# Sixteen score products and sixteen value products of the sample rows, one behind each K tile of the last two input blocks

## The chip, the cores and the metric

The kernel runs on one core of one Trainium2 chip. The metric is device time in microseconds, the median of three runs before. A profile of one execution stands beside it.

## The reference

One step of a hybrid decoder layer in fp32. A prompt (512 tokens behind 16 meta tokens) and eight sample rows share all weights. What matters here:

```python
z = h @ w_in + b_in                       # q (16 heads x 64) | k, v (4 x 64 each) | pool input u (1024)
# sample rows: one new token each against 128 cached keys and itself, with a sink per head
s = einsum('...qhgd,...shd->...hgqs', q, k_all) / 8
p = softmax over keys and the sink
a_s = einsum('...hgqs,...shd->...qhgd', p, v_all)
# prompt: the same in banded blocks of 128 queries; pool branch: trailing means of u over 2, 4, 8, 16, a linear map per group
h = LN(alpha*h + concat(attn, pool) @ w_o);  h = LN(alpha*h + SwiGLU(h))
```

## The kernel before

All dense products are made in three parts: a weight tile is split into `wh` and `wl` (ScalarE copies to fp32r, VectorE subtracts), activations likewise, and `products` (L200 to L206) issues wh x hi, wh x lo and wl x hi as fp32r matmuls, on lines 203, 204 and 206. `full_block` runs one block of 128 output columns over 16 K tiles: four groups of four, each group behind its own split. It holds two outputs, the two halves of the 536 token columns (276 and 260), so a K tile is six matmuls. With `apart=True` it runs all 16 K tiles for the first half and then all 16 for the second; only u7 does so.

The input stage makes k and v first and then eight q blocks (`q0` to `q7`, `q_block`) and eight pool blocks (`u0` to `u7`, `u_block`), in the order written in `order`. Between the blocks stand the steps of the prompt's attention: at each turn t of the loop at the end of the stage `att_values(t - 1)` (tile o, L609), `att_scores(t)` (tile sc, L547), the softmax on VectorE and ScalarE, then the block, then `att_turn(t)` (transposes of the probabilities, tile tp, L591 to L598). `pool_group` (tile pm) is the pool branch's linear map. `u_block` yields behind its block and VectorE's chain (u7 once more, between its two halves); called again, it transposes the last columns of u for an output (tile tpu, L657 and L658).

`with step(pe)` puts everything that TensorE gets inside it behind the step before. Inside a step, and on the other engines and on SP's queue, the order is settled by the planner that the kernel is built with, by program order, a priority for weight loads and splits, and its own estimate of what is ready.

`sample_attention` is a generator in stages, called with `next(sample)` at fixed places:

1. before u6: loads the K cache (`kc`, two loads), makes 16 score products (tile smT, L697: weights 128x128 of the cache, 8 columns moving), copies them out (L699);
2. behind u6 and `att_turn(6)`: transposes the scores (tile smp, L708, L709) and makes the softmax;
3. before u7: transposes the probabilities (tile smpt, L729, L730), copies them to pT (L732), loads the V cache (`vc`, two loads);
4. behind u7 and `att_turn(7)`: 32 value products in 16 pairs (tile smo, L742: weights 128x64 of the cache, 4 columns moving, the two of a pair on different halves of the output's partitions), and the sum (L748);
5. copies the result into the first eight columns of `mixf`, the operand of the output projection.

These products are plain fp32; each shows as two records on TensorE. The loads of weights and caches share a ring of five buffers (`raw`, `NRAW = 5`), taken in turn: kc, kc, u6, u6, pool group 2, vc, vc, u7, u7, pool group 3, w_o. PSUM has eight banks; the code asks for tags `mm` (2), `sc` (4), `pt` (1) and `o` (1), and the tool that lays out the tiles may give a tag another bank when one is free.

Of the kernel before, what the change touches and what calls it, by code (L numbers as in the profile page):

```python
# [16 lines left out]
KT = D // P  # L17
# [50 lines left out]
def hybrid_step(ctx, tc, xin, w_in, w_o, w_g, w_u, w_d, w_pool, par_d, cst_d, ident_d, ln2gb, kct_d, vc_d, hist_d,  # L68
# [136 lines left out]
        for j, o in enumerate(out):  # L205
            nc.tensor.matmul(o, wl, hi[j], start=False, stop=last, skip_group_check=onto)  # L206

    def full_block(src, name, out, hi, lo, low=None, apart=False):


        def mm(w, g, js):
            for kk in range(4):
                k = g * 4 + kk
                sl = slice(kk * P, (kk + 1) * P)
                products([out[j] for j in js], w[0][:, sl], w[1][:, sl], [hi(k)[j] for j in js], [lo(k)[j] for j in js],
                         k == 0, k == KT - 1)

        js = list(range(len(out)))
        ws = []
        for h in range(2):  # L220
            raw = load_raw(src[:, h * 1024:(h + 1) * 1024], f"{name}_{h}")
            for g in range(2):
                ws.append(split(raw[:, g * 512:(g + 1) * 512], f"{name}_{h}{g}", low))
                mm(ws[-1], 2 * h + g, js[:1] if apart else js)
        if apart:
            for g in range(4):
                mm(ws[g], g, js[1:])
# [27 lines left out]
    with ExitStack() as sa:  # L255
# [6 lines left out]
        def aux_tile(shape, tag, name, bufs):  # L262
            return ps.tile(shape, F32, tag=tag, name=name, bufs=bufs)
# [84 lines left out]
        xlo = [act.tile([P, KT, xw[h]], F32R, name=f"xlo{h}") for h in range(2)]  # L348
# [32 lines left out]
                y = y[:, :, META:]  # L381
            last.append(nc.sync.dma_start(h_d[ks, :, HALF[h]].rearrange("k p c -> p k c"), y).ins)

        def in_block(i, name, c0=0, apart=False):

            halves, cs = (0, 1), (slice(c0, xw[0]), slice(0, xw[1]))
            out = [mm_tile(f"mm_{name}_{h}")[:, cs[h]] for h in halves]
            full_block(w_in[i], name, out, lambda k: [xhi[h][:, k, cs[h]] for h in halves],
                       lambda k: [xlo[h][:, k, cs[h]] for h in halves], apart=apart)
            return out  # L390

        def rope(z, dst, name, c0=0):
# [43 lines left out]
        out = kv_banks(0)  # L436
# [4 lines left out]
        for h in range(2):  # L441
            for g in range(4):
                n = h * 4 + g + 1
# [27 lines left out]
            with step(*three):  # L471
# [6 lines left out]
                if h == 0:  # L478
                    out = kv_banks(1)
# [131 lines left out]
            nc.vector.tensor_copy(mixf[t][:, NS:NTOK], o.rearrange("p a b -> p (a b)"))  # L611


        def u_block(ub, apart=False):


            w = 2 << (ub // 2)
            hist = pa.tile([P, NS, POOLH], F32, tag="hist", name=f"hist{ub}", bufs=2)
            with tc.issue_after(last[-1]):
                nc.sync.dma_start(hist, hist_d[ub])  # L620
            out = in_block(12 + ub, f"u{ub}", apart=apart)
            u = pa.tile([P, C_ALL], F32, tag="u", name=f"u{ub}", bufs=2)
            bias = par[:, PBIAS + 12 + ub:PBIAS + 13 + ub]
            cur = [u] + [zt_tile(f"ws{ub}_{i}") for i in range(ub // 2 + 1)]
            if apart:
                d = pa.tile([P, NTOK], F32, name=f"d{ub}")
            else:
                d = zt_tile(f"d{ub}")
            dh = pa.tile([P, NTOK], F32R, tag="dh", name=f"dh{ub}", bufs=3)
            dl = pa.tile([P, NTOK], F32R, tag="dl", name=f"dl{ub}", bufs=3)  # L630
            dd[ub] = dh, dl
            for h, (c0, c1) in enumerate(((C_P, XN), (XN, C_ALL)) if apart else ((C_P, C_ALL),)):
                if h == 0:
                    nc.vector.tensor_scalar(u[:, NS:C_P], out[0][:, 0:META], bias, None, op0=ALU.add)
                    nc.vector.tensor_scalar(u[:, 0:NS], out[0][:, C_S:C_P], bias, None, op0=ALU.add)
                    nc.vector.tensor_scalar(u[:, C_P:XN], out[0][:, C_P:XN], bias, None, op0=ALU.add)
                if c1 == C_ALL:
                    nc.vector.tensor_scalar(u[:, XN:C_ALL], out[1], bias, None, op0=ALU.add)
                for i in range(1, len(cur)):
                    sh = 2 ** (i - 1)  # L640
                    a = c0 if h else NS + 2 ** i - 1
                    nc.vector.tensor_add(cur[i][:, a:c1], cur[i - 1][:, a:c1], cur[i - 1][:, a - sh:c1 - sh])
                nc.vector.scalar_tensor_tensor(d[:, c0 - META:c1 - META], cur[-1][:, c0:c1], 1.0 / w, u[:, c0:c1],
                                               op0=ALU.mult, op1=ALU.subtract)
                if h == 0:
                    hs = pa.tile([P, NS], F32, tag="hs", name=f"hs{ub}", bufs=2)
                    nc.vector.tensor_reduce(out=hs, in_=hist[:, :, POOLH + 1 - w:POOLH], op=ALU.add, axis=AX.X)
                    nc.vector.tensor_add(hs, hs, u[:, 0:NS])
                    nc.vector.scalar_tensor_tensor(d[:, 0:NS], hs, 1.0 / w, u[:, 0:NS], op0=ALU.mult, op1=ALU.subtract)
                ds = slice(c0 - META if h else 0, c1 - META)  # L650
                nc.scalar.copy(dh[:, ds], d[:, ds])
                nc.vector.tensor_sub(dl[:, ds], d[:, ds], dh[:, ds].bitcast(F32))
                if c1 < C_ALL:
                    yield
            yield
            tp = aux_tile([P, 512], "pt", f"tpu{ub}", 1)
            nc.tensor.transpose(tp[:POOLH, 0:P], u[:, C_ALL - POOLH:C_ALL], ident)  # L657
            nc.tensor.transpose(tp[:NS, P:2 * P], u[:, 0:NS], ident)  # L658
            uo = pa.tile([P, 2, P], F32, tag="uo", name=f"uo{ub}", bufs=1)
            nc.scalar.copy(uo[:POOLH, 0], tp[:POOLH, 0:P])  # L660
            nc.scalar.copy(uo[:NS, 1], tp[:NS, P:2 * P])
            us = slice(ub * P, (ub + 1) * P)
            nc.sync.dma_start(npp[:, us], uo[0:POOLH, 0, :])
            nc.sync.dma_start(nps[:, POOLH - 1, us], uo[0:NS, 1, :])
            yield
# [22 lines left out]
        def sample_attention():  # L688

            kcs = [load_raw(kct_d[:, 1024 * i:1024 * (i + 1)], f"kc{i}").rearrange("p (b t s) -> p b t s", b=4, t=2)  # L690
                   for i in range(2)]
            st_ = aux_tile([P, 2, 8, NS], "pt", "smT", 1)
            for b in range(NS):
                kc = kcs[b // 4][:, b % 4]
                for t4 in range(2):
                    ts = slice(4 * t4, 4 * t4 + 4)
                    nc.tensor.matmul(st_[:, :, ts, b], kc[:, t4, :], qd[:, :, ts, b], start=True, stop=True)  # L697
            sT = pa.tile([P, 2, 64], F32, tag="smT", name="sT")
            nc.scalar.copy(sT.rearrange("p j n -> p (j n)"), st_.rearrange("p j t b -> p (j t b)"))  # L699
            prod = pa.tile([P, 8, NS], F32, tag="smp", name="prod")  # L700
# [27 lines left out]
            for j in range(2):  # L728
# [3 lines left out]
            nc.scalar.copy(pT.rearrange("p j t b -> p (j t b)"), pp[:, 0:192])  # L732
            vcs = [load_raw(vc_d[:, 1024 * i:1024 * (i + 1)], f"vc{i}").rearrange("p (b f) -> p b f", b=4)
                   for i in range(2)]
            yield
            so = aux_tile([P, 8, NS], "pt", "smo", 1)
            for b in range(NS):
                vc = vcs[b // 4][:, b % 4]
                for t4 in range(2):
                    for j in range(2):  # L740
                        kv = 2 * t4 + j
                        nc.tensor.matmul(so[64 * j:64 * j + 64, 4 * t4:4 * t4 + 4, b], vc[:, kv * 64:kv * 64 + 64],  # L742
                                         pT[:, j, 4 * t4:4 * t4 + 4, b], start=True, stop=True)
            sv = pa.tile([P, 8, NS], F32, tag="sv", name="sv")
            for i in range(2):
                ts = slice(4 * i, 4 * i + 4)
# [8 lines left out]
        pe = nc.tensor  # L755
        qs, us = {}, []

        def block(n):
            with step(pe):
                if n[0] == "q":  # L760
                    qs[int(n[1])] = q_block(int(n[1]))
                else:
                    us.append(u_block(int(n[1]), n == "u7"))
                    next(us[-1])

        sample = sample_attention()
# [3 lines left out]
        for t in range(8):  # L770
            with step(pe):
                if t:
                    att_values(t - 1)
                sc = att_scores(t, qs.pop(t))
                if t >= 6:
                    next(sample)
            att_softmax(t, sc)
            done, us = us, []
            names = order[t].split()
            block(names[0])  # L780
            with step(pe):
                if t < 7:
                    att_turn(t)
                for u in done:
                    next(u)
                if t == 6:
                    next(sample)
            if t in (3, 5, 6):
                with step(pe):
                    next(pool_group((t - 2) // 2))  # L790
            for name in names[1:]:
                block(name)
        with step(pe):
            att_turn(7)
            next(sample)
        g3 = pool_group(3, True)
        for p in range(2):
            with step(pe):
# [338 lines left out]
    pe = nc.tensor  # L1137
# [387 lines left out]
```

## Time and profile before

| | |
|---|---|
| median of 3 runs | 1921.79 us (1921.46 to 1921.79) |
| the profiled execution | 1923.03 us |
| its span, first to last instruction | 1921.2 us |
| TensorE (PE) busy | 1890.5 us, 98% |
| VectorE (DVE) busy | 1537.7 us, 80% |
| ScalarE (ACT) busy | 957.6 us, 50% |
| mean granted TensorE clock | 0.993 |
| score products (smT) | 295.3 to 299.8 us |
| u6 | 299.8 to 314.0 us |
| u7 | 324.2 to 336.1 us |
| value products (smo) | 338.2 to 340.1 us |

A row of a timeline reads: start, duration (both us), engine, line, operation, output <- input by the program's names, rows*columns of the array used, shape of what moves, count; neighbours of one kind are merged into one row. PE is TensorE's products, PEld its weight loads, which run beside products; SPq is SP's queue of DMAs. A matmul's duration is modelled and contains its way through the array, so consecutive ones overlap; the distance from start to start tells what one costs.

### The profile page before, as it was taken

Reading aid. Unit: us, or ns where it says so; the run is one execution under the profiler, and the core shown is the slowest. Engines: PE = TensorE matmul, PEld = TensorE weight load, DVE = VectorE, ACT = ScalarE, POOL = GpSimd, SP = SyncE. Lnnn points to the kernel's source line nnn. Section 1 sums busy time; section 2 is a strip of 40 time slices with the busy share of each in tenths; the row PEclk is TensorE's granted clock in tenths of the full one; section 3 lists DMA queues with packets and bytes.
Section 4 is the critical chain, followed back from the end, with each engine's and each line's share of the span. In section 5 each row is a group of like instructions: output and inputs, shape, how many; then the busy total and the mean of one; then the engine's idle time right before and its main releaser. Section 6 shows DMA issues by size and latency. Waiting matters only on the chain.

```text
span 1921.2 us, 39215 instructions
## 1 busy us (share of the span) xinstructions
PE 1890.5 (98%) x15533; PEld 1862.9 (97%) x15533; DVE 1537.7 (80%) x2734; ACT 957.6 (50%) x1808; POOL 2.7 (0%) x9
## 2 busy tenths in 40 slices
PE   8999999999999999999999999999999999999996
PEld 8999999999989999999999999999999999999996
DVE  6666667768777988988898888888877888888878
ACT  6644445545654555555555555555555433434341
POOL 0000000000000000000000000000000000000000
PEclk9999999999999999999999999999999999999998
DMA  8722222665745455454545344453568655645332
GB/s 281 233 99 68 70 75 71 206 207 193 251 153 176 150 171 172 148 183 145 176 149 172 128 164 151 153 169 127 178 243 322 233 197 178 219 166 191 94 100 90
DMA packets 145240, 319.27 MB, mean 166 GB/s; under 512 B 14288, under 2 KB 66232, under 8 KB 144952
## 3 DMA queue, kind: packets, MB, share of 16 engines
q1 hardware_dynamic: 144480, 315.71, 49.6%
q8 instruction: 122, 2.00, 0.4%
q10 hardware_dynamic: 576, 1.05, 0.2%
q14 instruction: 62, 0.51, 0.1%
HBM read 265.22 MB, written 54.03 MB: 166 GB/s over the span
## 4 chain that ended last, share of the span: by engine, by line
PE 92%; DVE 3%; DMA 2%; ACT 2%; issue 1%; SPq 0%; DVEq 0%; ACTq 0%
PE p_g L203 8%; PE p_g L204 8%; PE p_g L206 8%; PE p_u L203 7%; PE p_u L206 7%; PE p_u L204 7%; PE tri L203 6%; PE tri L206 6%; PE tri L204 6%; PE o L203 3%; PE o L206 3%; PE o L204 3%; PE p_u L1003 2%; PE mm_u L203 2%; PE mm_u L206 2%; PE mm_u L204 2%
## 5 line engine op out<-in xcount | busy, mean ns | idle before, releaser
L187 ACT CAST rr<-fr 128x512 fp32r<-128x512 f32 (+1 forms) x1056 | 669.9, 644 | 738.3 <-DVE fr L196 151.5
L188 DVE TENSOR_TENSOR rr<-fr,rr 128x512 fp32r<-128x512 f32 (+1 forms) x1056 | 743.7, 715 | 244.2 <-ACT rr L187 233.8
L196 DVE TENSOR_TENSOR fr<-fr 128x1024 f32<-128x1024 f32 (+1 forms) x304 | 319.2, 1050 | 4.9 <-DMA fr<-in_w_g_dram 4.3
L203 PE MATMUL p_g<-rr 128*128 128x260 f32 x830 | 234.1, 283 | 0.0
L206 PE MATMUL p_g<-rr 128*128 128x260 f32 x830 | 230.2, 282 | 0.0
L204 PE MATMUL p_g<-rr 128*128 128x260 f32 x788 | 221.4, 282 | 0.0
L203 PE MATMUL p_u<-rr 128*128 128x260 f32 x770 | 217.8, 283 | 0.6 <-ACT fr L1044 0.6
L206 PE MATMUL p_u<-rr 128*128 128x260 f32 x770 | 214.7, 281 | 0.0
L204 PE MATMUL p_u<-rr 128*128 128x260 f32 x748 | 210.5, 282 | 0.0
L206 PE MATMUL tri<-rr 128*128 128x260 f32 x696 | 196.7, 283 | 1.8 <-DVE rr L188 1.8
L203 PE MATMUL tri<-rr 128*128 128x260 f32 x696 | 197.1, 283 | 0.8 <-ACT rr L187 0.8
L204 PE MATMUL tri<-rr 128*128 128x260 f32 x696 | 196.7, 283 | 0.0
L203 PEld LDWEIGHTS p_g<-rr 128*128 128x128 f32 x830 | 156.1, 188 | 0.0
L206 PEld LDWEIGHTS p_g<-rr 128*128 128x128 f32 x830 | 155.1, 189 | 0.0
L204 PEld LDWEIGHTS p_g<-rr 128*128 128x128 f32 x788 | 148.1, 188 | 0.0
L203 PEld LDWEIGHTS p_u<-rr 128*128 128x128 f32 x770 | 144.8, 188 | 0.8 <-ACT fr L1044 0.8
L203 PE MATMUL o<-rr 128*128 128x260 f32 x512 | 145.0, 284 | 0.3 <-ACT rr L187 0.3
L206 PEld LDWEIGHTS p_u<-rr 128*128 128x128 f32 x770 | 144.4, 189 | 0.0
L204 PE MATMUL o<-rr 128*128 128x260 f32 x512 | 144.0, 282 | 0.0
L206 PE MATMUL o<-rr 128*128 128x260 f32 x512 | 143.6, 282 | 0.2 <-DVE rr L188 0.2
L204 PEld LDWEIGHTS p_u<-rr 128*128 128x128 f32 x748 | 140.6, 188 | 0.0
L206 PEld LDWEIGHTS tri<-rr 128*128 128x128 f32 x696 | 131.3, 189 | 2.6 <-DVE rr L188 2.6
(320 smaller groups left out, 4563.2 us busy)
## 6 DMA issues: line engine op xcount, KB each, us to landing
fr<-in_w_u_dram SPq DMA_DIRECT2D x100, 512.0 KB
fr<-in_w_g_dram SPq DMA_DIRECT2D x90, 512.0 KB
fr<-in_w_d_dram SPq DMA_DIRECT2D x64, 640.0 KB
t_d<-fr SPq DMA_DIRECT2D x140, 260.0 KB
fr<-in_w_o_dram SPq DMA_DIRECT2D x64, 512.0 KB
fr<-in_w_in_dram SPq DMA_DIRECT2D x48, 512.0 KB
rr<-t_d SPq DMA_DIRECT2D x87, 260.0 KB
mid_b<-t_d SPq DMA_DIRECT2D x53, 260.0 KB
```

What stands on the lines that cost most here:

```text
L187: nc.scalar.copy(wh, s)
L188: last_lo[0] = (lo or nc.vector).tensor_sub(wl, s, wh.bitcast(F32)).ins
L196: i = op(*args).ins
L203: nc.tensor.matmul(o, wh, hi[j], start=first, stop=False, skip_group_check=onto)
L204: nc.tensor.matmul(o, wh, lo[j], start=False, stop=False, skip_group_check=onto)
L206: nc.tensor.matmul(o, wl, hi[j], start=False, stop=last, skip_group_check=onto)
L1003: nc.tensor.matmul(bk, self.q(0, n - 1)[:, k * P:(k + 1) * P], z1[0][4 * (n - 1) + k // 2][:, k % 2, :], start=(k == 0), stop=(k == 7))
```

## The change

The generator yields after every single score product, and after every pair of value products, and `full_block` gets an argument `side`: it calls `next(side)` behind each K tile. u6 and u7 pass the generator. In u6 the 16 calls issue one score product each. In u7, which has 32 calls, the first 16 meet bare yields (`KT + 1` of them, the first for the call ahead of the block), and the second 16 issue one pair of value products each. The copy of the scores and the sum of the values follow in a call behind the block. The loads of the K cache stay ahead of u6, those of the V cache ahead of u7 in program order. Because the value products now come inside u7, the tail transposes of u6 (tpu) move: from behind u7 to ahead of it, behind the transposes of the probabilities. `att_turn(7)` no longer has the value products behind it.

```diff
-    def full_block(src, name, out, hi, lo, low=None, apart=False):
+    def full_block(src, name, out, hi, lo, low=None, apart=False, side=None):
...
                 products([out[j] for j in js], w[0][:, sl], w[1][:, sl], [hi(k)[j] for j in js], [lo(k)[j] for j in js],
                          k == 0, k == KT - 1)
+                if side is not None:
+                    next(side)
...
             kcs = [load_raw(kct_d[:, 1024 * i:1024 * (i + 1)], f"kc{i}").rearrange("p (b t s) -> p b t s", b=4, t=2)
                    for i in range(2)]
+            yield
             st_ = aux_tile([P, 2, 8, NS], "pt", "smT", 1)
             for b in range(NS):
                 kc = kcs[b // 4][:, b % 4]
                 for t4 in range(2):
                     ts = slice(4 * t4, 4 * t4 + 4)
                     nc.tensor.matmul(st_[:, :, ts, b], kc[:, t4, :], qd[:, :, ts, b], start=True, stop=True)
+                    yield
...
-            yield
+            for _ in range(KT + 1):
+                yield
             so = aux_tile([P, 8, NS], "pt", "smo", 1)
             for b in range(NS):
...
                         nc.tensor.matmul(so[64 * j:64 * j + 64, 4 * t4:4 * t4 + 4, b], vc[:, kv * 64:kv * 64 + 64],
                                          pT[:, j, 4 * t4:4 * t4 + 4, b], start=True, stop=True)
+                    yield
...
-                    us.append(u_block(int(n[1]), n == "u7"))
+                    us.append(u_block(int(n[1]), n == "u7", sample if n in ("u6", "u7") else None))
...
             names = order[t].split()
+            if t == 7:
+                with step(pe):
+                    for u in done:
+                        next(u)
             block(names[0])
+            if t >= 6:
+                next(sample)
             with step(pe):
                 if t < 7:
                     att_turn(t)
-                for u in done:
-                    next(u)
+                    for u in done:
+                        next(u)
                 if t == 6:
                     next(sample)
...
         with step(pe):
             att_turn(7)
-            next(sample)
```

`in_block` and `u_block` hand `side` on.

More of the change, by code (lines that the diff above doesn't have):

```diff
@@ L382, in x_split, with in_block @@
             last.append(nc.sync.dma_start(h_d[ks, :, HALF[h]].rearrange("k p c -> p k c"), y).ins)
-        def in_block(i, name, c0=0, apart=False):
+        def in_block(i, name, c0=0, apart=False, side=None):
             halves, cs = (0, 1), (slice(c0, xw[0]), slice(0, xw[1]))
@@ L388, in in_block @@
             full_block(w_in[i], name, out, lambda k: [xhi[h][:, k, cs[h]] for h in halves],
-                       lambda k: [xlo[h][:, k, cs[h]] for h in halves], apart=apart)
+                       lambda k: [xlo[h][:, k, cs[h]] for h in halves], apart=apart, side=side)
             return out
@@ L611, in att_values, with u_block @@
             nc.vector.tensor_copy(mixf[t][:, NS:NTOK], o.rearrange("p a b -> p (a b)"))
-        def u_block(ub, apart=False):
+        def u_block(ub, apart=False, side=None):
             w = 2 << (ub // 2)
@@ L620, in u_block @@
                 nc.sync.dma_start(hist, hist_d[ub])
-            out = in_block(12 + ub, f"u{ub}", apart=apart)
+            out = in_block(12 + ub, f"u{ub}", apart=apart, side=side)
             u = pa.tile([P, C_ALL], F32, tag="u", name=f"u{ub}", bufs=2)
```

## The prediction

> **What bounds the kernel now.** I read the page's first and fourth part, then the granted clock by stage, then, record by record, the two stretches that the change edits.
>
> ```profile
> span 1921.2 us, 39215 instructions
> ...
> PE 1890.5 (98%) x15533; PEld 1862.9 (97%) x15533; DVE 1537.7 (80%) x2734; ACT 957.6 (50%) x1808; POOL 2.7 (0%) x9
> ...
> PE 92%; DVE 3%; DMA 2%; ACT 2%; issue 1%; SPq 0%; DVEq 0%; ACTq 0%
> ```
>
> TensorE is busy for 98% of the span and carries 92% of the chain that ended last, so a microsecond added to or taken from its order near 300 us moves the end by about as much. The windows view tells where its clock is not full; its columns are the stretch, busy time of PE, PEld, DVE, ACT and POOL, PEclk, DMA share and GB/s.
>
> ```profile
> 294.50:297.90 3.40, 3.40 (x34) 3.02 (x30) 3.40 (x18) 0.81 (x3) 0.00 (x0) 1.00 0.28 102
> 297.90:301.30 3.40, 3.40 (x18) 3.40 (x18) 3.33 (x14) 3.40 (x16) 0.00 (x0) 0.51 0.64 167
> 301.30:304.80 3.50, 3.50 (x17) 3.50 (x17) 1.64 (x7) 1.08 (x6) 0.00 (x0) 0.50 0.38 137
> ...
> 338.90:342.30 3.40, 3.40 (x61) 2.73 (x59) 3.40 (x14) 0.54 (x2) 0.00 (x0) 1.00 0.53 156
> 342.30:345.70 3.40, 3.40 (x27) 2.84 (x26) 3.40 (x15) 2.72 (x8) 0.00 (x0) 0.50 0.88 266
> ```
>
> The clock falls to a half twice: for some 6.8 us from 297.9, just behind a stretch of score products (smT), and for 3.4 us from 342.3, behind a stretch with the value products (smo). "Busy" stays full in both stretches before; what is small there is the work in the array: 8 or 4 columns a product. These two runs are what the change breaks up. The Trainium skill, page "TensorE: Matmul & The Clock Gate", Part 1, says that the clock is full or half and is decided over windows of about 3.4 us of activity. The trace agrees: stretches of two such lengths and of one, at 0.50.
>
> **The change part by part.** No product, copy or load is added or removed. Each term is what TensorE's order gains (-) or loses (+), against this profiled execution.
>
> First the score products. The tile view, the windows of that tile and of u6's products, and the timeline:
>
> ```profile
> L697 PE MATMUL smT<-fr x32: 256/256/362, 295.3 to 299.6; 128*128 128x8 f32 x32
> 295.30:297.90 2.60, 2.60 (x24) 2.60 (x24) 0.00 (x0) 1.00 0.10 39
> 299.78 0.58 PE L203 MATMUL mm_u<-rr 128*128 128x276 f32 x1
> 300.15 0.43 PE L204 MATMUL mm_u<-rr 128*128 128x276 f32 x1
> 300.10:304.70 4.60, 4.60 (x22) 4.60 (x22) 0.00 (x0) 0.50 0.42 126
> 305.00:309.60 4.60, 4.60 (x39) 4.60 (x39) 0.00 (x0) 1.00 0.22 61
> ```
>
> (a) The run goes: 299.78 - 295.30 = 4.48 us, and the first big product's interval of 0.37 comes down by 0.15 to the 0.22 that a first product takes elsewhere (340.14 to 340.36, below): -4.63.
> (b) The half clock behind it goes. At half clock 4.6 us hold 22 records less one or two at the edges, 0.22 us apart; at full clock 39 less two, 0.124. The work of those 4.6 us takes 2.55 at full clock: -2.05.
> (c) The sixteen products come back, one behind each K tile of u6, two records each. In the run at full clock a record takes 2.60 us / 23.3 = 0.112 whatever its 8 columns, so it is the weight load that is paid. Behind a big product the first load hides under that product, but the next big product's load no longer hides under anything longer than 8 columns: two loads are exposed per insertion, as in the run. 16 x 2 x 0.112 = +3.58. From below, the loads could hide altogether (some 0.2 us in all); from above, each could pay the switching of (e), +6.6. I take 3.58, since shapes and tile (128*128) are those of the run and of the products around.
>
> Score products together: -3.10.
>
> Then the value products, whose weights are 128*64:
>
> ```profile
> 319.30 0.28 PE L206 MATMUL pm<-rr 128*128 128x260 f32 x1
> 319.51 2.82 PE L609 MATMUL o<-mid_a 16*64 16x128 f32 x32
> 322.26 1.82 PE L547 MATMUL sc<-mid_a 64*128 64x152 f32 x16
> 337.97 0.27 PE L598 MATMUL tp<-fr,mid_a 128*128 128x128 f32 x1
> 338.17 0.23 PE L742 MATMUL smo<-fr 128*64 128x4 f32 x2
> L742 PE MATMUL smo<-fr x64: 199/199/220, 338.2 to 340.0; 128*64 128x4 f32 x64
> 340.01 0.20 PE L742 MATMUL smo<-fr 128*64 128x4 f32 x1
> 340.14 0.39 PE L203 MATMUL pm<-rr 128*128 128x260 f32 x1
> 340.36 0.28 PE L204 MATMUL pm<-rr 128*128 128x260 f32 x1
> ```
>
> (d) The run goes: from the last transpose at 337.97 to the second big product at 340.36 are 2.39 us; without it a big product behind a transpose and its successor take 0.24 (346.07, 346.10 and 346.31, next fence): -2.15.
> (e) Inside the run a record costs only 1.84 us / 63 = 0.029, since two halves of the array load in turn. Alone behind a K tile each group of four records pays for getting in and out. In: a 64-column product behind a big one starts 0.21 after it (319.30 to 319.51) where a big one follows after 0.12. Four records: 3 x 0.029 = 0.09. Out: 0.13 (340.01 to 340.14), and the first big product holds its successor for 0.22. 0.21 + 0.09 + 0.13 + 0.22 = 0.65 where two big products take 0.24: 0.41 per insertion, sixteen of them in u7's second pass: +6.6. From below, four records at the run's pitch (0.12) with no switching: +1.9; from above, 0.35 in as at half clock (344.40 to 344.76 is such a switch the other way): +8.8. I take 6.6, as each part of it has a row of this shape or of this switch.
>
> (f) The second half-clock stretch goes.
>
> ```profile
> 341.06 3.78 PE L609 MATMUL o<-mid_a 16*64 16x128 f32 x30
> 344.40 0.43 PE L609 MATMUL o<-mid_a 128*64 128x128 f32 x2
> 344.76 0.80 PE L203 MATMUL pm<-rr 128*128 128x260 f32 x2
> 345.50 0.53 PE L609 MATMUL o<-mid_a 128*64 128x128 f32 x2
> 346.07 0.27 PE L658 MATMUL tpu<-fr,mid_a 128*8 128x128 f32 x1
> 346.10 0.37 PE L204 MATMUL pm<-rr 128*128 128x260 f32 x1
> 346.31 0.28 PE L206 MATMUL pm<-rr 128*128 128x260 f32 x1
> ```
>
> The 32 products of att_values took 2.75 us at full clock (319.51 to 322.26); here 30 take 3.70 (341.06 to 344.76), the first 1.2 us of it still at full clock: about -0.5 (the first ones, which stood at full clock, are slower here than there as well, and I do not count that). The two pm and two o from 344.76 to about 346.1, at half clock with two switches between: about -0.6. Together -1.1. Bounds: 0 if the stretch only moves elsewhere, -1.7 if all 3.4 us run at twice the speed.
>
> (g) What moves on other engines, at nothing:
>
> ```profile
> L699 ACT COPY fr<-smT x1: 244/244/244, 302.1 to 302.1; 128x128 f32<-128x128 f32 x1
> 313.96 0.27 PE L591 MATMUL tp<-fr,mid_a 128*16 128x128 f32 x1
> 315.93 0.38 PE L708 MATMUL smp<-fr 128*64 128x128 f32 x2
> 316.56 0.25 ACT L660 COPY fr<-tpu 15x128 f32<-15x128 f32 x1
> 297.29 3.00 SPq L180 DMA_DIRECT2D fr<-in_vc_dram  x2
> 339.31 1.29 SPq L180 DMA_DIRECT2D fr<-in_w_o_dram  x2
> ```
>
> The copy of the scores (0.24 us, at 302.1) now comes behind u6; its reader L708 starts 1.97 us after u6's end (313.96 to 315.93), behind att_turn's transposes. Without that cover it would cost the copy and its signals, at most 0.6. Tail transposes of u6 move ahead of u7, right behind the transposes of the probabilities. Both ask for the tag "pt" with one buffer; yet L708 wrote at 315.93 what was to be a buffer that ACT read only at 316.56, so the two had different banks, and I count no wait. On SP, the loads of the cached values (vc) were issued when the K cache's slots came free, at 297.29 and some 3 us later; now those come free in the middle and at the end of u6. Their readers are in u7's second pass, more than 15 us on; u7's own weights were read before them. The first columns of w_o take the slots of vc: they were issued at 339.31, behind the run of smo; now they come up to 5 us earlier relative to u7's end. DVE and ACT get some 6 us more beside u7 for their splits and u7's chain, and lose 3 us behind it: no new wait.
>
> Sum: -4.63 - 2.05 + 3.58 - 2.15 + 6.6 - 1.1 = +0.25 us. The profiled execution took 1923.03 us for its span of 1921.2, 1.24 over the median of the runs shown, 1921.79. I lay the difference on that median: 1922.0. What the change wins with the clock it pays back by switching the array 16 times between 128*128 and 128*64.
>
> **A rule weighed.** Row: 0.21 from a big product to a 64-column one, 0.13 back. The Trainium skill, same page, Part 2, says that TensorE pulls a weight load ahead of products in flight when it targets the background weight buffer. By that rule alone the in and out of (e) would hide, 0.09 and about 0.1 of each 0.41; that is rival 2. The rows of 128*128 agree with the rule, those of 64 columns do not.
>
> **The rivals.**
> 1 (slower). The clock gate closes in u7's second pass. A product of 260 columns occupies the array for about 0.108 us (at half clock, where nothing else limits it, the products of u6 follow at 0.22). A K tile there is three of them, 0.36 us, and 0.41 for the insertion, so they fill the array for 3 x 0.108 / 0.77 = 42%, over 12 us. How full must it be? Ahead of the first dip only the score products (sc) up to 295.30 fill it, 0.8 of 3.4 us, 24%; ahead of the second I estimate 28%: six pm products, and ten records of o that use 64 columns and partly 16 rows. The next row, 12 transposes of 0.11 us in 3.4 us, 38%, kept its clock:
>
> ```profile
> 14.60:18.00 3.40, 1.81 (x12) 1.30 (x12) 1.49 (x5) 2.01 (x3) 0.00 (x0) 1.00 1.01 365
> ```
>
> So it speaks for a limit between 28% and 38%, and 42% passes, narrowly; it decides if the insertion takes over 0.5 us or the measure is another. At half clock a K tile takes about 0.65 + 0.58 = 1.23 instead of 0.77; closed from one to two windows in, for 7 to 12 K tiles: +3.4 to +5.5, and up to 1 in the tail: about 1926.5.
> 2 (cheaper switching). In and out of (e) hide: 16 x 0.19 = 3.0 less: 1919.0. Against it, the rows of (e).
> 3 (the second dip stays). A window of u7's last K tiles, the 16 transposes of att_turn(7) and little else could close the gate again: no gain in (f), 1923.1. The skill's page, Part 4, says that transposes do not count as busy for the gate, which would make this likely; the row above, with nothing but transposes at clock 1.00, speaks against it.
> 4 (not what it says). The order is settled by a planner; if it packs the small products into gaps ahead, both runs and their dips partly stay and little is paid: 1919 to 1922.
>
> **How the numbers follow.** Forecast 0.53 (1922.0, own range 1919.5 to 1924.5); rival 1 0.20, rival 2 0.09, rival 3 0.10, rival 4 0.08. A measurement can tell about 0.2%, 3.8 us, from no change. Rival 1 lies above 1925.6 in three cases of four, 0.15, and mis-sized terms of the others add 0.04: slower 0.19. Faster needs (e) near its lower end with all else as forecast: 0.08. Same 0.73. The range takes in rival 2 with a better tail and most of rival 1: 1917.5 to 1926.8.
>
> **What would show it.** After the change: PEclk 1.00 from 290 to 350 (right), or 0.50 in u7's second pass (rival 1) or behind it (rival 3). smT records in pairs behind each K tile of u6, and about 0.97 us per K tile instead of 0.74; smo records in fours in u7's second pass with 0.77 per K tile, starting 0.21 behind the big product. L708 and u6's tail transposes without a wait. The prediction is wrong if an insertion of smo takes under 0.2 or over 0.55 us, if the clock falls in u7, or if out_proj starts on a wait of its own.

## The result and the profile after

The changed kernel takes 1924.85 us, median of 20 runs (1921.97 to 1927.86), against 1921.19 for the kernel before in the same comparison (20 runs, 1917.15 to 1922.98). The ratio is 1.0021, with a 95% interval from 1.0015 to 1.0028: slower by 3.66 us. Forecast were 1922.0 and a range of 1917.5 to 1926.8. The profiled execution after took 1924.52 us, close to its median; the profiled execution before had taken 1923.03, which is 1.84 above the median of these 20 runs and above the longest of them. So the two profiles differ by only 1.49 us where the runs differ by 3.66, and that is one of the two things to explain; the other is where the profile itself departs from the forecast.

The page of the changed kernel, its first and fourth part:

```profile
span 1922.7 us, 39215 instructions
...
PE 1891.0 (98%) x15533; PEld 1861.4 (97%) x15533; DVE 1538.8 (80%) x2734; ACT 957.2 (50%) x1808; POOL 2.7 (0%) x9
...
PE 92%; DVE 4%; DMA 2%; ACT 2%; issue 1%; SPq 0%; ACTq 0%; DVEq 0%
```

TensorE is still the bound, with the same number of instructions. The windows view by stage (stretch, busy time of PE, PEld, DVE, ACT and POOL, PEclk, DMA share, GB/s): u6, the tail transposes with u7's first pass, u7's second pass, and what stands behind u7.

```profile
295.30:310.80 15.50, 15.50 (x130) 15.43 (x129) 9.58 (x39) 7.03 (x25) 0.00 (x0) 1.00 0.28 86
322.40:329.70 7.30, 7.00 (x53) 6.59 (x53) 5.62 (x26) 6.69 (x28) 0.00 (x0) 1.00 0.05 18
329.70:341.40 11.70, 11.70 (x110) 9.36 (x109) 7.72 (x23) 5.66 (x14) 0.00 (x0) 1.00 0.27 91
341.40:350.00 8.60, 8.60 (x81) 7.38 (x82) 7.80 (x26) 7.34 (x22) 0.00 (x0) 1.00 0.56 177
```

The clock is 1.00 in all four: both half-clock stretches of the profile before are gone. The timeline shows the insertions, in u6 and in u7's second pass:

```profile
296.20 0.28 PE L700 MATMUL smT<-fr 128*128 128x8 f32 x2
296.34 0.37 PE L203 MATMUL mm_u<-rr 128*128 128x276 f32 x1
296.55 0.29 PE L204 MATMUL mm_u<-rr 128*128 128x276 f32 x1
...
297.17 0.28 PE L700 MATMUL smT<-fr 128*128 128x8 f32 x2
...
330.50 0.29 PE L747 MATMUL smo<-fr 128*64 128x4 f32 x4
330.71 0.39 PE L203 MATMUL mm_u<-rr 128*128 128x260 f32 x1
330.94 0.28 PE L204 MATMUL mm_u<-rr 128*128 128x260 f32 x1
331.06 0.28 PE L206 MATMUL mm_u<-rr 128*128 128x260 f32 x1
331.27 0.29 PE L747 MATMUL smo<-fr 128*64 128x4 f32 x4
```

From one insertion to the next are 0.97 us in u6 (296.20 to 297.17) and 0.77 in u7 (330.50 to 331.27), the two pitches that the prediction gave. What it did not give is this, at the start of u7 (the number in brackets is the idle time before the instruction, with what released it):

```profile
320.78 0.28 PE L733 MATMUL smpt<-fr 64*128 64x64 f32 x2
320.89 0.22 PE L734 MATMUL smpt<-fr 64*128 64x64 f32 x1
322.41 0.28 PE L659 MATMUL tpu<-fr,mid_a 128*15 128x128 f32 x1 [1.29 <-DVE fr L564]
322.53 0.27 PE L660 MATMUL tpu<-fr,mid_a 128*8 128x128 f32 x1
323.09 0.39 PE L203 MATMUL mm_u<-rr 128*128 128x276 f32 x1 [0.29 <-DVE fr L564]
```

u6's tail transposes (tpu), moved ahead of u7, wait for L564, the part of the softmax in which VectorE reads the scores of turn 7, and then u7's first product waits for it again. Two of these reads, the second and the fourth of the last four, end just ahead of the two starts, at 322.34 and 323.03:

```profile
321.92 0.42 DVE L564 CUSTOM_DVE_ANT_0 mid_a<-sc,fr 128x256 f32<-128x256 f32 x1
322.61 0.42 DVE L564 CUSTOM_DVE_ANT_0 mid_a<-sc,fr 128x256 f32<-128x256 f32 x1
```

u7 starts 2.20 us behind the last transpose of the probabilities (320.89 to 323.09). In the profile before it started 0.15 behind it:

```profile
324.04 0.22 PE L730 MATMUL smpt<-fr 64*128 64x64 f32 x1
324.19 0.39 PE L203 MATMUL mm_u<-rr 128*128 128x276 f32 x1
```

The order of TensorE, mark by mark, in the two profiled executions (us):

| stretch | before | after | difference | predicted |
|---|---|---|---|---|
| start to last score product of turn 6 | 295.00 | 295.06 | +0.06 | 0 |
| from there to att_turn(6), with u6 | 18.96 | 15.75 | -3.20 | -3.10 |
| from there to the last smpt | 10.08 | 10.07 | -0.01 | 0 |
| from there to u7's first product | 0.15 | 2.20 | +2.05 | +0.22, moved |
| u7, its first product to the next work behind it | 11.93 | 18.40 | +6.47 | +6.6 |
| from there to the third column of the output projection | 29.42 | 25.68 | -3.75 | -3.47 |
| from there to the end | | | -0.05 | 0 |

The sum is +1.58 against +0.25 forecast, 1.33 more. One row alone has 1.83 us of waiting that the forecast had not; the others together come out 0.5 us better than forecast.

### The profile page after: what moved, and what is told of

Its sections match the earlier page's. It is cut to its first block, busy times and chain, and to the rows that moved or that the text cites. A ratio compares the mean times of both kernels' runs of the same rounds, so it can differ in the third digit from the quotient of the medians.

```text
span 1922.7 us, 39215 instructions
## 1 busy us (share of the span) xinstructions
PE 1891.0 (98%) x15533; PEld 1861.4 (97%) x15533; DVE 1538.8 (80%) x2734; ACT 957.2 (50%) x1808; POOL 2.7 (0%) x9
## 4 chain that ended last, share of the span: by engine, by line
PE 92%; DVE 4%; DMA 2%; ACT 2%; issue 1%; SPq 0%; ACTq 0%; DVEq 0%
PE p_g L203 8%; PE p_g L204 8%; PE p_g L206 8%; PE p_u L203 7%; PE p_u L206 7%; PE p_u L204 7%; PE tri L203 6%; PE tri L206 6%; PE tri L204 6%; PE o L203 3%; PE o L206 3%; PE o L204 3%; PE p_u L1014 2%; PE mm_u L203 2%; PE mm_q L203 2%; PE mm_u L206 2%
```

## The experiments

The theory after this reading: the switching (the way from products of 128 columns to products of 64 and back) costs what was forecast, the wait of tpu and u7 comes from PSUM banks, and the rest of the timed difference comes from the kernel before, which does not lose both half-clock stretches in every execution. The rivals: the switching or the wait is something else (a V cache that arrives late, VectorE's load); or something behind the output projection is slower. The last of these is settled for the two profiles by the table: from the third column to the end they differ by 0.05 us. And TensorE's only waits between 300 and 375 us of the changed kernel are those of tpu and u7; none ends with a DMA. Four kernels were run together on one chip, beside the kernel before with 1920.84 us (median of 30 runs, 1916.08 to 1923.64). The edits that follow are shown against the changed kernel unless another is named, and in part.

**The kernel before again.** No edit; its profile is a second look at the same program.

> The kernel before, unchanged, to see the granted clock of each execution. Theory A (the change cost more on the clock of time, about 3.7 us, than between the two profiles, 1.6 us, because the half-clock stretches of before depend on where the clock's windows fall and are not in every execution): the mean clock of the executions varies, some near 0.996 with none or one stretch and shorter by 1 to 4 us, others at 0.993 with both; ratio 1.000. Rival R (the stretches of before are in every execution, and the extra loss is u7's second pass falling to half clock in some executions of the changed kernel): every execution of before at 0.993, within 1 us of each other.

Measured: 1921.06 us (11 runs, 1920.13 to 1922.18), ratio 1.0002 (0.9993 to 1.0010). Its mean clocks run from 0.992 to 0.995, and the times differ by 2 us: neither all alike nor, as the theory expected of some, at 0.996. Of the 30 executions beside it one, the shortest at 1916.08, has 0.997. Its profile, windows first and then rows of the timeline:

```profile
294.90:299.50 4.60, 4.60 (x42) 4.32 (x39) 4.57 (x25) 2.53 (x11) 0.00 (x0) 1.00 0.39 105
299.50:304.00 4.50, 4.50 (x39) 4.50 (x38) 3.58 (x13) 3.29 (x13) 0.00 (x0) 1.00 0.56 172
334.60:338.00 3.40, 3.40 (x76) 3.06 (x74) 3.40 (x11) 1.17 (x3) 0.00 (x0) 1.00 0.49 155
338.00:344.80 6.80, 6.80 (x40) 4.90 (x39) 6.80 (x26) 5.59 (x16) 0.00 (x0) 0.50 0.93 271
```

```profile
295.18 3.74 PE L697 MATMUL smT<-fr 128*128 128x8 f32 x32
298.78 0.37 PE L203 MATMUL mm_u<-rr 128*128 128x276 f32 x1
```

The run of score products is all there, 295.18 to 298.78, yet no half clock stands behind it; behind the value products it lasts two windows instead of one. So the first stretch is no property of the program alone: it depends on where the gate's windows lie when the run comes. The half-clock stretches here are 3.4 or 6.8 us long, and one in a later run 34.1, ten times as long as the shortest: a window is 3.41 us. An estimate from that: counted back twelve windows from 338.0, where this execution's clock falls, an edge lies at 297.0 and cuts the run into 1.85 and 1.75 us, with other products beside each; in the execution before, the window from 294.5 to 297.9 held 2.6 us of it. With the clock full, the stretch with u6 takes 15.83 us, and interleaved 15.75: without its half clock, the run costs the same as the insertions to 0.1 us. The Trainium skill, page "TensorE: Matmul & The Clock Gate", Part 1, says that the gate's window runs freely and does not start with the kernel; these two executions of one program agree: 6.8 us of half clock at 297.9 in the one and none there in the other.

**The score products alone.** Only u6 takes the generator along; the run of value products and tpu stay where they were before.

```diff
-            for _ in range(KT + 1):
-                yield
+            yield
...
-                    us.append(u_block(int(n[1]), n == "u7", sample if n in ("u6", "u7") else None))
+                    us.append(u_block(int(n[1]), n == "u7", sample if n == "u6" else None))
...
         with step(pe):
             att_turn(7)
+            next(sample)
```

> Only the score products go behind u6's K tiles; the value products stay in a run behind att_turn(7), and u6's tail transposes stay behind u7. Theory A: in the profile u6's stretch from the last score record to the first transpose falls from 18.96 to about 15.8 us, -3.2 against the profile of before; on the clock of time a gain of 1 to 3 us, since at full clock a product behind a K tile costs what it costs in the run (0.224 us). Rival R: the full 3.2 us, ratio 0.9983.

Measured: 1918.15 us (11 runs, 1916.99 to 1920.36), ratio 0.9983 (0.9974 to 0.9991). Against the same kernel before, its interval and that of the change (1.0015 to 1.0028) lie on different sides of 1. A gain of 1 to 3 us was expected, the full 3.2 by the rival; 2.7 does not tell them apart.

```profile
295.40:311.20 15.80, 15.80 (x132) 15.47 (x131) 9.86 (x41) 7.04 (x25) 0.00 (x0) 1.00 0.29 91
335.20:337.20 2.00, 2.00 (x65) 1.83 (x63) 2.00 (x7) 1.06 (x3) 0.00 (x0) 1.00 0.33 125
337.20:344.00 6.80, 6.80 (x70) 5.63 (x67) 6.80 (x26) 4.04 (x11) 0.00 (x0) 1.00 0.77 234
```

u7 starts 0.15 us behind smpt. The value run is there (335.2 to 337.2, 65 records) and in this execution no half clock follows it, so its profile shows the old order behind u6 with no dip at all: from att_turn(7) to the third column of the output projection 27.97 us, where one window of half clock makes 29.21 (before) and two make 30.65 (before again). A window there costs 1.24 to 1.44 us. One execution each shows this; the mean clocks of this kernel's other runs, 0.994 to 0.996 against 0.996 in the profile, suggest that some of them lose a window or two somewhere.

**The value products alone.** Only u7 takes the generator along; the score run stands ahead of u6 as before, tpu ahead of u7 as in the change.

```diff
-            yield
             st_ = aux_tile([P, 2, 8, NS], "pt", "smT", 1)
...
-                    yield
             sT = pa.tile([P, 2, 64], F32, tag="smT", name="sT")
...
-                    us.append(u_block(int(n[1]), n == "u7", sample if n in ("u6", "u7") else None))
+                    us.append(u_block(int(n[1]), n == "u7", sample if n == "u7" else None))
```

> Only the value products go behind the K tiles of u7's second pass, with u6's tail transposes ahead of u7; the score products stay in a run before u6. Theory A: u7 takes about 18.4 us instead of 11.9 (+6.5), a wait of up to 1.8 for a bank ahead of u7, and 3.5 to 3.8 less behind u7: +3 to +5 us, ratio 1.0016 to 1.0026. Rival R adds the half clock in u7's second pass in some executions: +5 to +8, ratio over 1.0026.

Measured: 1926.62 us (8 runs, 1924.89 to 1927.66), ratio 1.0030 (1.0019 to 1.0040): more than the 3 to 5 us expected, with an interval that holds both the theory's figures and the rival's.

```profile
294.70:298.90 4.20, 4.20 (x38) 3.87 (x36) 4.20 (x22) 2.08 (x10) 0.00 (x0) 1.00 0.39 97
298.90:302.30 3.40, 3.40 (x17) 3.40 (x17) 2.49 (x11) 3.21 (x14) 0.00 (x0) 0.51 0.67 227
330.00:343.00 13.00, 13.00 (x120) 10.53 (x120) 9.01 (x27) 6.29 (x17) 0.00 (x0) 1.00 0.25 82
```

This execution has the first dip with one window (u6's stretch 17.37 us, against 15.83 and 18.96), the full clock in u7, and the wait again, 2.35 us from smpt to u7. The halves add up as the change does within their intervals: -2.7 and +5.8 make +3.1.

**The tail transposes early.** The change, but tpu goes ahead of `att_values(6)`, before the scores of turn 7 are made.

```diff
+                if t == 7:
+                    for u in us:
+                        next(u)
...
-            if t == 7:
-                with step(pe):
-                    for u in done:
-                        next(u)
             block(names[0])
```

> The changed kernel with the tail transposes of u6 ahead of att_values(6) instead of behind the scores of turn 7, so that they and u7 need not ask for a bank that VectorE is still reading. Theory A: the wait between the transposed probabilities and u7's first product (2.20 us in the changed kernel's profile) falls to about 0.15, so 1.8 to 2.0 us less than the changed kernel: +1.5 to +2.2 us against before, ratio 1.0008 to 1.0012. Rival R: the wait was hidden by slack behind u7 and the gain is under 0.5 us: ratio 1.0018 or more.

Measured: 1922.82 us (11 runs, 1921.99 to 1924.85), ratio 1.0014 (1.0005 to 1.0023).

```profile
321.28 0.22 PE L734 MATMUL smpt<-fr 64*128 64x64 f32 x1
321.43 0.40 PE L203 MATMUL mm_u<-rr 128*128 128x276 f32 x1
```

u7 follows smpt by 0.15 us: the wait is gone, and up to att_turn(7) nothing takes its place (u7 itself 17.97 us to its last product, as in the change). From att_turn(7) to the third column of the output projection it is 0.6 us longer than in the change; there the planner has att_values(7) in three pieces instead of two. The span is 1.8 us shorter than that of the change (1920.9 against 1922.7); by the ratios to the kernel before it saves 1.3, but their intervals overlap, so the trace shows the wait gone and the times alone do not show the gain. The layouts of PSUM in the built programs say why. In the change, the four score tiles of turn 7 have banks 6, 7, 0 and 1; tpu has bank 0, that of the third, and u7's first output bank 1, that of the fourth, and VectorE was still reading both (L564). Before, the scores had banks 1, 2, 5 and 6, tpu came behind u7 in bank 0, and u7 had banks 3 and 4; with tpu early it has bank 5 and u7 bank 4, none of them awaited.

What stays is the switching. The next kernels, run together on another chip (before: 1920.72, median of 21 runs), change its size.

**Value products of full width.** The kernel with tpu early; in place of two products of 128x64 weights a pair becomes one of 128x128 weights with 8 columns, of whose output half is read.

```diff
...
-                    for j in range(2):
-                        kv = 2 * t4 + j
-                        nc.tensor.matmul(so[64 * j:64 * j + 64, 4 * t4:4 * t4 + 4, b], vc[:, kv * 64:kv * 64 + 64],
-                                         pT[:, j, 4 * t4:4 * t4 + 4, b], start=True, stop=True)
+                    ts = slice(4 * t4, 4 * t4 + 4)
+                    nc.tensor.matmul(so[:, :, ts, b], vc[:, t4 * P:(t4 + 1) * P], pT[:, 0:2, ts, b], start=True, stop=True)
...
```

> As tail_early, but each pair of value products of two heads is one product with 128x128 weights and eight columns; the halves of its output that mix heads are left unread. Theory A (an insertion of the 64-column products pays 0.2 us for switching the array's columns in and out): a K tile of u7's second pass takes 0.36 + 2 x 0.112 = 0.58 us instead of 0.77, u7 about 15.0 instead of 18.0: 3 us less than tail_early, 1919.8, ratio 0.9995. Rival (an insertion costs what it costs because plain fp32 stands among fp32r, whatever its columns): K tile still 0.77, ratio 1.0014.

Measured: 1919.89 us (11 runs, 1918.09 to 1922.53), ratio 0.9993 (0.9984 to 1.0002), against 1.0014 (1.0005 to 1.0023) for the same kernel with narrow products: 4 us less, with some 2.4 us of uncertainty, where u7 got 2.8 shorter. The profiled execution was the slowest of the 11. First the timeline in u7's second pass, then windows at the start of this kernel and, in the fence behind, the second of them in the kernel with narrow products:

```profile
330.46 0.28 PE L746 MATMUL smo<-fr 128*128 128x8 f32 x2
330.60 0.37 PE L203 MATMUL mm_u<-rr 128*128 128x260 f32 x1
330.80 0.28 PE L204 MATMUL mm_u<-rr 128*128 128x260 f32 x1
330.93 0.28 PE L206 MATMUL mm_u<-rr 128*128 128x260 f32 x1
331.04 0.28 PE L746 MATMUL smo<-fr 128*128 128x8 f32 x2
```

```profile
14.60:18.00 3.40, 1.60 (x12) 1.31 (x12) 1.59 (x6) 1.80 (x3) 0.00 (x0) 1.00 1.05 386
18.10:24.80 6.70, 5.42 (x24) 5.24 (x23) 5.33 (x10) 6.67 (x13) 0.00 (x0) 0.50 1.02 349
```

```profile
18.10:24.80 6.70, 5.37 (x42) 5.06 (x41) 5.32 (x9) 6.67 (x13) 0.00 (x0) 1.00 1.03 361
```

A K tile with the same multiplications takes 0.58 us instead of 0.77 (330.46 to 331.04), and u7 15.16 instead of 17.97 to its last product: of the insertion's price of 0.41, 0.19 was the narrow tile and its four records in place of two, not that the insertion is small or alone. The start behind the big product falls from 0.21 to 0.11 (330.93 to 331.04). Two records fewer account for no more than 0.06, at the 0.03 that a record costs in a run. What the next big product holds its successor for, 0.20 (330.60 to 330.80), hardly changes and so is no matter of the tile. At the start of the kernel nothing was edited, and yet this execution ran 6.7 us at half clock there, and came to u6 1.3 us later than the other. Half-clock stretches come and go there too; the window ahead of this one, 14.6 to 18.0 with 12 products, is the same that kept its clock in the prediction.

**The value run between u7's two passes.** The kernel with only the score products interleaved; the value products stay a run, but between the passes. The edit is shown against the kernel before.

```diff
...
+        if mid is not None:
+            next(mid)
...
-            next(sample)
         g3 = pool_group(3, True)
```

> As scores_alone, with the run of value products between the two passes of u7, dense products on both sides, instead of behind att_turn(7). Theory A: the run keeps its price of about 2.1 us, no window of the clock is filled by it and little else, so no half clock near 340: 0 to 1.4 us less than scores_alone, ratio 0.9976 to 0.9983. Rival (the half clock moves with the run): a stretch at 0.50 inside u7's second pass in the profile, 2 us or more slower than scores_alone.

Measured: 1919.53 us (11 runs, 1918.16 to 1920.58), ratio 0.9991 (0.9983 to 1.0000).

```profile
327.72 2.03 PE L748 MATMUL smo<-fr 128*64 128x4 f32 x64
329.69 0.39 PE L203 MATMUL mm_u<-rr 128*128 128x260 f32 x1
```

```profile
335.50:345.00 9.50, 9.00 (x73) 7.54 (x71) 9.50 (x26) 8.39 (x24) 0.00 (x0) 1.00 0.48 168
```

The waits of TensorE in that window (engine, tile and line waiting, what released it: total, times, longest, us):

```profile
PE o L204 <- DVE rr L838: 0.3, 1, 0.3
PE pm L203 <- DVE mid_a L642: 0.2, 1, 0.2
```

In one piece the 64 records cost u7 2.16 us (13.97 against 11.81), where sixteen insertions cost 6.5 (18.40 against 11.93, each to the next work behind u7): it is the getting in and out sixteen times that is paid. The move itself brings nothing to be seen: the stretch behind u7 gets only 1.38 shorter (26.59 against 27.97), as TensorE now idles 0.5 us there on VectorE's splits and sums, which the run had covered. The time is 1919.53 against 1918.15 for the run behind u7, 1.5 more by the ratios, whose intervals overlap; 0 to 1.4 less had been expected, and the rival's half clock in u7's second pass is not in this profile. It has one window of it at 20.0 us and one at 50.7 instead, which no edit touched.

**Each value product twice, and four times.** The kernel with tpu early, with each of the 32 products issued again, so that the big products fill a smaller part of u7's second pass. One execution each. For the kernel with four times the products the loop reads `range(4)`.

```diff
...
+                        for _ in range(2):
...
```

> As tail_early, with every value product issued twice (same result), to see how little of the array's time big products may fill before the clock falls. Big products then fill about 0.324/0.89 = 37% of u7's second pass. Theory A (limit between 28% and 38%): undecided, most likely full clock, a K tile of 0.89 us. Rival (the limit lies just under the 42% of the changed kernel): half clock from one or two windows into the pass, K tiles of about 1.3 us.

> As tail_early, with every value product issued four times: big products fill about 0.324/1.12 = 29% of u7's second pass. Theory A: the clock falls to a half in the pass, K tiles of 1.5 to 1.7 us there. Rival (the clock looks at whether products follow each other, not at how full they are): full clock, 1.12 us.

Measured: 1929.02 and 1945.86 us. Twice first, then four times:

```profile
329.40:332.80 3.40, 3.40 (x45) 2.90 (x44) 3.40 (x11) 1.34 (x3) 0.00 (x0) 1.00 0.00 0
332.80:336.20 3.40, 3.40 (x45) 2.77 (x44) 2.40 (x7) 1.35 (x4) 0.00 (x0) 1.00 0.65 211
336.30:349.80 13.50, 13.50 (x89) 11.71 (x89) 6.40 (x23) 5.81 (x15) 0.00 (x0) 0.50 0.34 116
```

```profile
329.20:332.50 3.30, 3.30 (x53) 2.99 (x52) 2.92 (x11) 1.00 (x3) 0.00 (x0) 1.00 0.00 0
332.60:366.70 34.10, 34.10 (x259) 31.02 (x258) 13.28 (x41) 9.71 (x26) 0.00 (x0) 0.50 0.25 84
```

With the products doubled a K tile takes 0.89 us at full clock, so by the prediction's measure (three products in it, each an estimated 0.108 us, half of the 0.22 that they take at half clock) the array is 36% full. By that measure the first full window of the pass, up to 332.8, holds 38% (12 products begin in it), and the clock stays; the next holds 35% (11 products), and behind it the clock is at a half, for four windows (336.3 to 349.8), with K tiles of 1.48 us. Full clock had been expected as the likelier, and half clock at 1.3 us by the rival. With four times the products a K tile takes 1.37 us at full clock, which makes 24%, and a single window is enough; at half clock it takes 2.35. Expected were 1.12 and 1.5 to 1.7; why these records cost more than 0.03 us each was not found. This is the prediction's first rival, made to happen.

## Why the prediction was right and where it failed

The time lies inside the range, 2.85 us above the forecast and 0.35 above the likeliest case's own range. That it lies inside is in part luck: the upper end of the range had been set for rival 1, which did not happen. As a difference the forecast was +0.2 and the measurement +3.66. The balance that was described, a clock won back and paid out in switching, is what the profile shows; a wait and the usual size of what was won back were missed. Step by step:

(a), (b) and (c), the score products. Forecast -3.10, in the two profiles -3.20. An insertion costs the forecast 0.224 us (a K tile of 0.97). But the term is the size of one execution: of the 3.2 us, all but 0.1 is the half clock (15.83 without it, 17.37 with one window, 18.96 with two), and that stretch is not in each execution.

(e), the insertions of value products. Forecast +6.6; the profile has +6.47, the K tile of 0.77 to the hundredth. The products of full width bear out that the tile is paid for: with the tile of the neighbours a K tile is 0.19 us shorter, the 0.09 and about 0.1 that rival 2 gave for in and out, though up to 0.06 of it may be the two records fewer. Rival 2 (the switching hides) is refuted for 64 columns, and holds for 128.

(d) and (f), what goes behind u7. The value run without any dip was worth 2.29 us there (27.97 with the score products alone, 25.68 after), forecast 2.15; the one window of half clock 1.24, forecast 1.1. With tpu, which moved, -3.75 against -3.47. As with (b), the dip's size is right for that execution.

The term that was mis-sized is the clock in (b) and (f), once the sum is laid on the median. The prediction took the difference of one pair of executions for that of the medians, with 4.4 us lost to half clock in the one before (3.13 and 1.24). The score products alone, with the old order behind u6 and neither dip in its profile, has 1918.15 as its median and took 1917.99 in the profiled execution; the kernel before stands 2.7 above that. So a usual execution of it loses nearer to 2.7 than to 4.4, an estimate that takes a usual execution of the other to be like its profiled one. The second profile of the kernel before fits: it lost 2.68 (30.65 against 27.97) and took 1920.75, near the median of 1920.84. From the last score product to the third column of the output projection the traces give 66.17 us for the kernel before without any half clock (15.83 + 10.08 + 0.15 + 11.93 + 27.97 + 0.21 for tpu) and 72.10 for the change: +5.9, and with 2.7 won back +3.2, against +3.66 measured. The hint was there: the profiled execution lay 1.24 above the median of the runs, and the prediction named it and used it for nothing. The timed difference is the profiles' 1.49, plus the 1.84 by which that execution lay above its median of 20 runs, plus the 0.33 by which the one after lay below its own: 3.66.

(g) failed: "I count no wait". The prediction asked if tpu and smp share a bank, found that they do not, and stopped. It did not ask which bank tpu would get in its new place and who still read that one. 1.83 us of waiting was the answer, in two banks of the scores of turn 7, tpu's and u7's. tpu ahead of those scores takes the wait away; that the banks were the cause rests on that, on the layouts and on the two reads of VectorE at whose ends the waits end.

The rivals: the clock held in u7's second pass (1.00 from 329.7 to 341.4), narrowly as the prediction said, with 38 to 44% of work in the windows (12 to 14 products begin in each). The limit lies at the upper end of the 28 to 38% that it gave: a window at 35% closed the gate, windows at 38% kept it open in u7's second pass. It is not sharp by this measure. The row that the prediction took it from, 12 transposes from 14.6 to 18.0, kept the clock in the profile before (1.00 behind it) and not in that of the products of full width (0.50 behind it). No run shows the rival's price of 1.23 us for a K tile at half clock; with the products doubled it was 1.48. Rival 3 did not happen: clock 1.00 from 341.4 to 350.0 behind 16 transposes. Rival 4 did not: the order is the one written.

Open: the timed runs of the change spread from 1921.97 to 1927.86 with clocks of 0.993 to 0.997, and only one of them has a trace. That one has no half clock between 290 and 350 us and a mean of 0.996; profiles with three windows of it (before, and the products of full width) have 0.993. So the four runs at 0.993, the three longest among them, lost about three windows by this estimate. Where, in u7's second pass or at the start of the kernel, was not seen. With tpu early, ten of eleven runs have 0.996 or 0.997 with the same insertions in u7, which speaks against the second pass and does not settle it.

## What to carry to other kernels

Before small products are put between big ones, look at their tile: with the tile of the neighbours an insertion cost here what its records cost in a run (0.224 us for two), with half the columns it cost the switch each time (0.41 us), and then a run was cheaper. When an operation with a PSUM tile moves forward, list the banks that are free at its new place and who reads them last, not only the bank it had. And a half-clock stretch in one profile is a chance, not a cost: compare the profiled execution with the runs, and weigh what its removal brings. Here the fastest version measured is a part of the change: the score products interleaved and the value run left alone, 0.9983 (0.9974 to 0.9991).

## What the runs showed of the hardware

The same program lost two windows of half clock behind the score products in one execution and none in the next, and one or two behind the value products; even the first 25 us, which no edit touched, had 6.7 us of it in one execution and none in another. TensorE was "busy" throughout behind the score and the value products: what counted here was how full the array was, with a limit between 35 and 38% of a window in u7's second pass by the estimate of 0.108 us a product. And products of 64 columns on either half of the array cost 0.03 us a record in a run, but took 0.21 us to enter from a full-width product (0.11 with full width), while full-width products of 8 columns came in for 0.112 us a record, which is what they cost in a run.
